# A two-layer trunk on one Trainium2 core: where the values' scale is computed, which queue issues attention's DMAs, and which tile holds a residual

## The chip, the cores and the metric

The kernel runs on one core of a Trainium2 chip. A core has five engines that run their own instruction streams in order and wait for each other by semaphores: TensorE (PE in the profile; PEld is its weight load), VectorE (DVE), ScalarE (ACT), GpSimd (POOL) and SyncE (SP). DMAs are issued by an engine's queue, here SP's or POOL's, and carried out by 16 DMA engines that all queues share. The metric is the device time of one execution in microseconds (us). Matrix products write to PSUM, eight banks, and everything else lies in SBUF or in device memory (DRAM).

## The reference

The function is a trunk of two residual layers over a sequence of 1024 tokens of width 1024, followed by a normalization:

```python
for i in range(DEPTH):                 # DEPTH = 2
    h = rms_norm(x, norm_g[i])
    x = x + (lru_mixer(h, ...) if i == 0 else fox_mixer(h, ...))
return rms_norm(x, final_g)
```

Layer 0 projects `h` to 2 x 1536 columns, runs a causal convolution of four taps, two block-diagonal gates of 12 blocks of 128, and a linear recurrence along the sequence, multiplies by a SiLU gate and projects back. Layer 1 is causal attention with 16 heads of 64 and a forget gate:

```python
u = h @ w_in                           # q, k, v, gate (1024 each), f_logit (16)
cum = cumsum(log_sigmoid(f_logit + b_f))
logits = (q . k) / 8 + cum[query] - cum[key], masked to key <= query
y = softmax(logits) @ v * silu(gate)
x = x + y @ w_out
```

All is float32 in the reference. The kernel keeps close to that by splitting each operand of a product into a high and a low part and adding three products.

## The kernel before, in words

**Tiling and precision.** Activations are held transposed: 128 channels in the partitions, 512 tokens (one half of the sequence) in the free dimension. A weight block is loaded as float32 into a staging tile `wf` (`loaded`, L103: three buffers, and during layer 0 a fourth, `wx`), ScalarE writes its high part `wh` (L88), and GpSimd or VectorE subtracts it to get the low part `wl` (L99); `wh` and `wl` have four buffers each. The staging buffer is free again once the low part is written. `split_weights` (L109) issues these loads on SP's queue (L112), in both layers.

**Layer 0** is a loop of twelve steps (L396 to L440). Step `n` projects one block of 128 recurrence channels, computes the gates of block `n - 1`, the gate branch, the recurrence, and fills in the output projection of earlier pairs of blocks. At its end (L465 to L489) the last pair is projected, the new residual `x1` goes to DRAM (`x1d`), and `rms_row` computes the second norm's row `rs1` and its column form `rms1`, for each half of the sequence.

**Layer 1** starts with the first pair of heads' keys and queries and the first group of values, then loops over 16 heads. A step for head `hd` has two runs: `weigh(hd, 0)` beside `maxima(hd, 1)`, and `weigh(hd, 1)` beside `maxima(hd + 1, 0)`; the second argument is the half of the queries.

- `maxima` (L717) does for each of four blocks of 128 queries: the scores S on TensorE, from a key tile `T[s]` and a query tile `U[s][c]`; mask and maximum on VectorE (L741); the exponential with its sum on ScalarE (L746); the sum divided by a constant on GpSimd (L752) and its reciprocal on VectorE (L753); the weights as two float16 parts `pp`, high on ScalarE (L90) and low on VectorE (L755); and a transposing DMA (L756) of `pp` into `pT[c]`, issued on SP's queue.
- `weigh` (L761) multiplies `pT[c]` by the values into O, once all four transposes have landed. The result is scaled by `tops` (L781 to L783), gated and stored to `y1d`.
- `load` and `load_q` (L624, L636) copy a head's keys and queries, within SBUF, into T and U, and rows of the forget gate from DRAM: four DMAs for T, four for each U, on SP's queue. T and the second U alternate between heads, the first U is shared by all.
- The projections of the next pair (keys, queries, gate) are the `fill` between these steps, six pieces of weights for a pair.
- After every fourth head, `values` (L541) computes the values of the next four heads. They are stored as two float16 parts, so they need a scale that can't overflow. `bound` (L523) finds it: for each of eight weight tiles ScalarE squares the high part times the norm's gain (L528), TensorE sums over partitions with a matrix of ones (`norms`, 128x256 in bfloat16), VectorE takes the maximum over the columns (L531), ScalarE takes a square root (L532), and VectorE derives the inverse, `rv` (L538), and the unit by which O is scaled back. The values' products go on meanwhile, but a finished product can be evicted (L90, L584) only with `rv`.

**The end** starts at head 12. `load_y` (L829) brings back the gated outputs of six pairs, `partial` (L857) multiplies them by the output weights and adds to the residual, which is loaded from `x1d` on SP's queue and stored back to it on GpSimd's (L869). `late` (L952) loads and splits the weights of the last two pairs. `turned` (L889) transposes the residual by TensorE, in quarters of 256 tokens, adds the last two pairs' product in the same PSUM tile, and normalizes. For its first quarter, `residual` (L875) loads into the home of `pT[0]` and the result goes to the home of the key tile `T[0]`.

**Order.** The program is written as generators that are interleaved by hand (`run`, L810, with the strings ORDER and LAST), TensorE's instructions being chained to that order. Within it a planner orders each engine's instructions ahead of time by its own estimate of their durations. On the chip every engine and every queue takes its instructions strictly in that order: an instruction that waits holds up all that is behind it on its engine, a DMA that waits all that is behind it on its queue.

Of the kernel before, what the change touches and what calls it, by code (L numbers as in the profile page):

```python
# [40 lines left out]
def trunk(ctx: ExitStack, tc: tile.TileContext, xt, w0, wg, wo0, pc, gn, gf, w1, wv, wf, bf, wo1, out):  # L41
# [10 lines left out]

    pe = [None]

    def matmul(*args, **kw):
# [15 lines left out]
    nc.vector.memset(tiny, 1e-30)  # L71
    onesb = const.tile([P, P], BF16, name="onesb")
    nc.vector.memset(onesb, 1.0)
    root = const.tile([P, 1], F32, name="root")
# [34 lines left out]
    def split_weights(src, shape, hi_eng, lo_eng, parts=wpool):  # L109
        wt = loaded(shape)  # L110
        for part, sl in src:
            nc.sync.dma_start(wt[:, :, sl], part)  # L112
# [73 lines left out]
    with ExitStack() as l0:  # L186
# [206 lines left out]


        ys, fill, held = [], iter(()), {}
        for n in range(NB):  # L396
            wu = first[0] if n == 0 else list(weights(w0[n]))
            if n == 1:
                ups = both = [ps.tile([P, HALF], F32, tag="g", name="ups") for h in range(2)]
            else:  # L400
                ups = two_banks("ups")
                both = [ups.rearrange("p a b -> p (a b)")]
                ups = [ups[:, h] for h in range(2)]
            product(ups[0], 0, wu)
            if n == 0:
                gps = held[0] = two_banks("gps")
                product(gps[:, 0], 0, first[1])
                for _ in zip(split_x(1), square_x(1)):
                    pass
                done = norm_row(0)  # L410
            else:
                gates(n - 1)
                if n > 1:
                    with tc.issue_after(state[n - 1]["last"].ins):
                        outputs(n - 2)
            product(ups[1], 1, wu)
            if n == 0:
                product(gps[:, 1], 1, first[1])
                norm_row(1)
# [38 lines left out]
        def mm3(o, w, x, start, stop):  # L458
# [3 lines left out]
            matmul(o, wh, xl, start=False, stop=stop)  # L462

        wl = [w for d0 in range(0, KT, 2) for w in out_weights(NB // 2 - 1, d0)]
        for h, cs in enumerate(halves):  # L465
# [4 lines left out]
            for d0 in range(0, KT, 4):  # L470
# [6 lines left out]
                for db, o in enumerate(pts, d0):  # L477
# [10 lines left out]
                    )  # L488
            rms_row(sums, rs1[h], rms1[h])  # L489


# [5 lines left out]
    with ExitStack() as l1:  # L497
# [24 lines left out]

        def bound(g, parts):  # L523

            row = ps.tile([P, HALF], F32, tag="O", name="norms")[:, :256]
            for k in range(KT):
                sq = at.tile([P, 256], BF16, tag="yo", name="sqw", bufs=2)
                nc.scalar.activation(sq, f32(parts[k][0][:, :256]), AF.Square, scale=gnt[:, 1, k : k + 1])  # L528
                matmul(row, onesb, sq, start=k == 0, stop=k == KT - 1)
            most = const.tile([P, 1], F32, name=f"most{g}")  # L530
            nc.vector.tensor_reduce(most, row, mybir.AxisListType.X, ALU.max)  # L531
            nc.scalar.activation(most, most, AF.Sqrt, bias=tiny, scale=SEQ / TOP / TOP)  # L532
            unit_ = tops[g] = const.tile([P, 1], F32, name=f"unit{g}")
            nc.vector.tensor_scalar(unit_, most, 0.5 / TOP, None, ALU.mult)
            nc.vector.reciprocal(most, most)
            rv = const.tile([P, 8], F32, tag="rv", name="rv", bufs=2)
            for h in range(2):
                nc.vector.tensor_scalar(rv[:, 4 * h : 4 * h + 4], rms1[h], most, None, ALU.mult)  # L538
            return rv

        def values(g):  # L541
# [17 lines left out]
            for st, k in todo:  # L559
# [19 lines left out]
                for a in range(2):  # L579
                    v = vpool.tile([P, 4, HD], FP16, tag=f"v{st}", name=f"v{st}", bufs=2)  # L580
                    src = pt[:, a * P : (a + 1) * P].rearrange("p (b d) -> p b d", b=2)
                    rv_ = rv[:, st : st + 1]
                    to_hi(v[:, 0::3], src, nc.scalar, scale=rv_)
                    nc.vector.scalar_tensor_tensor(v[:, 1:3], src, rv_, v[:, 0::3], ALU.mult, ALU.subtract)  # L584
                    Vs[2 * g + a].append(v)
                if ex:
                    nc.vector.tensor_scalar(fz[:, st], pt[:, 256:], r_, None, ALU.mult)

        tops = {}
        kq = {}  # L590
# [7 lines left out]
        def low(pair):  # L598
            return nc.vector if pair else nc.gpsimd

# [23 lines left out]
        def load(hd, cs=slice(0, SEQ), us=(0, 1)):  # L624

            pair, s = hd // 2, hd % 2
            rows = slice(s * HD, (s + 1) * HD)
            hi, lo = (f32(z[rows, cs]) for z in kq[pair, 1])
            nc.sync.dma_start(f32(T[s][:64, 0, cs]), hi)
            nc.sync.dma_start(f32(T[s][:64, 1, cs]), hi)  # L630
            nc.sync.dma_start(f32(T[s][64:, 0, cs]), lo)
            nc.sync.dma_start(f32(T[s][66:68, 1, cs]), cumd[hd, :, cs])
            for c in us:
                load_q(hd, c)

        def load_q(hd, c):  # L636
            s = hd % 2
            u = U[s][c]
            hi, lo = (f32(z[s * HD : (s + 1) * HD, halves[c]]) for z in kq[hd // 2, 0])
            nc.sync.dma_start(f32(u[:64, 0]), hi)  # L640
            nc.sync.dma_start(f32(u[64:, 0]), hi)
            nc.sync.dma_start(f32(u[:64, 1]), lo)
            nc.sync.dma_start(f32(u[64:66, 1]), cumd[hd, :, halves[c]])

# [72 lines left out]
        def maxima(hd, c):  # L717
# [7 lines left out]
            for i in range(4 * c, 4 * c + 4):  # L725
# [25 lines left out]
                r = sums[:, i : i + 1]  # L751
                nc.gpsimd.tensor_scalar(r, r, 1.0 / TOP, None, ALU.mult)  # L752
                nc.vector.reciprocal(r, r)  # L753
# [7 lines left out]
        def weigh(hd, c, sub=slice(0, HALF)):  # L761
# [18 lines left out]
            r0, r1 = s * HD, (1 - s) * HD  # L780
            to, one = yo[r0 : r0 + HD], tops[hd // 4]  # L781
            nc.scalar.activation(to, O[r1 : r1 + HD], AF.Copy, scale=one[r1 : r1 + HD])
# [3 lines left out]
        def gated(hd, c, sub=slice(0, HALF)):  # L786
# [42 lines left out]
        def load_y(c):  # L829
            for pair in range(6):  # L830
                nc.sync.dma_start(f32(pair_of_y(c, pair)[1]), y1d[c, pair])
            yield from ()
# [24 lines left out]
        def partial(todo):  # L857

            for db, c in todo:
# [15 lines left out]
        def residual(c, q):  # L875

            cs = slice(q * 256, (q + 1) * 256)
            if c == q == 0:
                xs = at.tile([P, KT, 256], F32, tag="pT0", name="x1", bufs=1)
                xs = [xs[:, d] for d in range(KT)]  # L880
                for d, x in enumerate(xs):
                    nc.sync.dma_start(x, x1d[c, :, d, cs])
                return xs
            xs = [wpool.tile([P, 2, 256], F32, tag=("wl", "wh")[q], name="x1") for d in range(4)]
            for d, x in enumerate(xs):
                nc.sync.dma_start(x, x1d[c, :, 2 * d : 2 * d + 2, cs])
            return [x[:, i] for x in xs for i in range(2)]

        def turned(c, q):  # L889
# [62 lines left out]
        def late():  # L952

            for half in range(2):
                wh, wl = (kqpool.tile([P, 8, P], F32R, tag=f"qk{p}{half}", name=f"wo{p}") for p in "hl")
                for b in range(2):
                    wt = wpool.tile([P, 4, P], F32, tag="wf", name="wf", bufs=3)
                    for d in range(2):
                        nc.sync.dma_start(wt[:, 2 * d : 2 * d + 2], wo1[half * 4 + b * 2 + d, :, 6:8])
                    sl = slice(4 * b, 4 * b + 4)  # L960
# [150 lines left out]
```

## Time and profile before

| what | time |
| --- | --- |
| median of three runs | 1130.51 us (1129.42 to 1133.2) |
| the profiled execution | 1140.27 us |
| its span, first to last instruction | 1138.5 us |
| mean granted TensorE clock in it | 0.975 |
| busy: TensorE / its weight loads | 1074.5 / 857.5 us |
| busy: VectorE / ScalarE / GpSimd | 761.8 / 624.9 / 151.9 us |
| DMA: 138.86 MB, of it on GpSimd's queue | 4.20 MB |

A page of the profile has the busy time of each engine, the span in 40 slices with a digit each for the busy tenths (and for the granted clock and the DMA engines' busy share), the DMA queues, the chain of work that ended last, and groups of instructions. A group's row reads: line, engine, operation, output<-inputs, shapes, count | busy us, mean ns of one | idle us before it and what ended that. A waits row reads: who waited <- for whom: total us, times, longest. A stretch's row has its bounds and length, then busy us and count for PE, PEld, DVE, ACT and POOL, then the granted clock, the DMA share and GB/s. Durations of matmuls are modelled and overlap, so a chain's spacing, not the mean of a group, tells what one costs. Layer 0 ends near 450 us; the heads run from some 510 to 1095 us.

### The profile page before, as it was taken

How to read it: one execution, taken by the hardware profiler on the slowest of the kernel's cores; microseconds unless marked ns; L12 is line 12 of the kernel's file. 1: busy time of each engine (PE TensorE's matmuls, PEld its weight loads, DVE VectorE, ACT ScalarE, POOL GpSimd, SP SyncE). 2: the span in 40 equal slices, each digit the busy share in tenths (PEclk: the TensorE clock that was granted, in tenths of full speed). 3: DMA queues.
4: the chain of work that ended last, by engine and by line, in shares of the span. 5: the costliest groups of instructions: out<-in, count | busy, mean ns of one | idle time of the engine just before them, and what ended most of it. 6: DMA issues, size and time to landing. Idle time of an engine off the chain costs nothing. (4 is left out here: it accounts for less than half of the span.)

```text
span 1138.5 us, 14931 instructions
## 1 busy us (share of the span) xinstructions
PE 1074.5 (94%) x5130; PEld 857.5 (75%) x5130; DVE 761.8 (67%) x1314; ACT 624.9 (55%) x1053; POOL 151.9 (13%) x215
## 2 busy tenths in 40 slices
PE   9999999999999999899898899988999889999887
PEld 7788888888888887787676776767767678667666
DVE  7888765677567789558767277772776726576445
ACT  8488344445543647367656366553665536554334
POOL 1321212212021102321010000100001000011100
PEclk9999999999999999999999999998999989999899
DMA  6111111111111114338989448893588933899784
GB/s 233 56 47 50 44 52 51 47 51 42 51 52 42 51 52 144 108 95 175 165 178 191 93 114 171 180 191 87 115 177 176 190 87 90 235 210 214 180 206 184
DMA packets 212610, 138.86 MB, mean 122 GB/s; under 512 B 160660, under 2 KB 175508, under 8 KB 212536
## 3 DMA queue, kind: packets, MB, share of 16 engines
q1 hardware_dynamic: 211256, 133.73, 49.8%
q0 software_dynamic: 1280, 4.20, 1.2%
q8 instruction: 40, 0.66, 0.2%
q14 instruction: 34, 0.28, 0.1%
HBM read 59.11 MB, written 15.86 MB: 66 GB/s over the span
## 5 line engine op out<-in xcount | busy, mean ns | idle before, releaser
L56 PE MATMUL gps<-hh,wh 128*128 128x512 f32 x576 | 236.5, 411 | 1.0 <-DVE qkl L620 1.0
L56 PE MATMUL gps<-hl,wh 128*128 128x512 f32 x576 | 229.0, 397 | 0.0
L56 PE MATMUL gps<-hh,wl 128*128 128x512 f32 x576 | 228.7, 397 | 0.0
L88 ACT CAST wh<-wf 128x512 fp32r<-128x512 f32 (+2 forms) x156 | 94.1, 606 | 141.5 <-PE ops L56 53.5
L99 POOL TENSOR_TENSOR wl<-wf,wh 128x512 fp32r<-128x512 f32 (+1 forms) x60 | 99.8, 1670 | 398.5 <-ACT wh L88 367.1
L56 PEld LDWEIGHTS gps<-hl,wh 128*128 128x128 f32 x576 | 109.6, 190 | 25.7 <-issue 0.5
L56 PEld LDWEIGHTS gps<-hh,wh 128*128 128x128 f32 x576 | 110.0, 191 | 25.2 <-DVE qkl L620 1.2
L746 ACT ACTIVATE p<-S,m 128x128 f32<-128x128 f32 (+7 forms) x128 | 94.4, 738 | 59.8 <-DVE sums L753 25.1
L56 PEld LDWEIGHTS gps<-hh,wl 128*128 128x128 f32 x576 | 110.1, 191 | 20.6 <-POOL wl L99 0.3
L755 DVE SCALAR_TENSOR_TENSOR pp<-p,sums,pp 128x128 f16<-128x128 f32 (+7 forms) x128 | 104.1, 814 | 28.1 <-ACT pp L90 27.2
L90 ACT ACTIVATE pp<-p,sums 128x128 f16<-128x128 f32 (+7 forms) x128 | 97.9, 771 | 27.2 <-DVE sums L753 9.1
L741 DVE CUSTOM_DVE_ANT_0 S<-S,mask 128x128 f32<-128x128 f32 (+7 forms) x128 | 97.3, 761 | 22.5 <-PE S L56 21.0
L752 POOL TENSOR_SCALAR sums<-sums 128x1 f32<-128x1 f32 x128 | 37.8, 295 | 497.2 <-ACT p L746 497.1
L56 PE MATMUL O<-pT,v 128*128 128x512 f16 (+3 forms) x396 | 83.2, 340 | 21.5 <-DMA pT<-pp 21.5
L56 PE MATMUL S<-T,U 96*128 96x512 f32 (+7 forms) x384 | 93.7, 353 | 3.7 <-ACT p L746 3.7
L56 PE MATMUL vps<-wh,hh 128*128 128x256 f32 (+1 forms) x256 | 76.9, 301 | 15.3 <-DVE v L584 11.7
L387 DVE TENSOR_TENSOR x<-x,ops 128x512 f32<-128x512 f32 x80 | 54.1, 683 | 48.5 <-PE ops L56 48.5
L56 PEld LDWEIGHTS <-v 128*128 128x128 f16 x396 | 33.2, 102 | 68.9 <-issue 37.4
L56 PEld LDWEIGHTS S<-T,U 128*128 128x128 f32 (+1 forms) x384 | 68.8, 190 | 19.7 <-ACT p L746 6.9
L56 PE MATMUL ups<-hl,wh 128*128 128x512 f32 x192 | 76.9, 401 | 0.1
L56 PE MATMUL ups<-hh,wh 128*128 128x512 f32 x192 | 76.4, 399 | 0.6 <-ACT hh L90 0.6
L56 PE MATMUL ops<-yh,wh 128*128 128x512 f32 x192 | 76.3, 398 | 0.5 <-DVE x L480 0.5
(185 smaller groups left out, 2105.8 us busy)
## 6 DMA issues: line engine op xcount, KB each, us to landing
wf<-in_w SPq DMA_DIRECT2D x100, 256.0 KB
wf<-in_wo SPq DMA_DIRECT2D x64, 128.0 KB
U<-qkh SPq DMA_DIRECT2D x64, 128.0 KB
T<-qkh SPq DMA_DIRECT2D x28, 256.0 KB
x<-in_xt SPq DMA_DIRECT2D x16, 256.0 KB
x1d<-x SPq DMA_DIRECT2D x16, 256.0 KB
wf<-in_wv SPq DMA_DIRECT2D x16, 256.0 KB
U<-qkl SPq DMA_DIRECT2D x32, 128.0 KB
```

Of the source, the lines that this page charges most:

```text
L56: pe[0] = nc.tensor.matmul(*args, **kw)
L88: nc.scalar.copy(hi, src)
L90: nc.scalar.activation(hi, src, AF.Copy, scale=scale)
L99: return eng.tensor_tensor(lo, src, f32(hi), ALU.subtract)
L387: nc.vector.tensor_tensor(x, x, pt, ALU.add)
L741: nc.vector.tensor_tensor_reduce(S[:, :n], S[:, :n], mask[:, SEQ - n :], -1.0, -NEG, ALU.add, ALU.min, accum_out=m)
L746: seen[0] = nc.scalar.activation(p, S[:, :n], AF.Exp, bias=m, scale=-1.0, accum_out=sums[:, i : i + 1])
L752: nc.gpsimd.tensor_scalar(r, r, 1.0 / TOP, None, ALU.mult)
L755: nc.vector.scalar_tensor_tensor(both[:, :, 1], p, r, both[:, :, 0], ALU.mult, ALU.subtract)
```

## The change

It has five parts.

1. The bound on the values leaves attention. In layer 0, steps 1 to 8 each load two pieces of the values' weights (`vsq`, 16 loads of 256 KB in all, on SP's queue, through the weights' staging buffers) and ScalarE squares each and sums it along the row. At the end of layer 0, `value_bounds` multiplies those sums by the larger of two squared gains, adds over partitions with one product of 128x128 by 128x16, takes the square root and derives `unit_v` and `scale_v` for all four groups; `rv` for all is made behind each half's `rms_row`. `bound` and its calls go, and the bfloat16 ones.
2. All loads of attention go through `fetch`. It is SP's queue until the first values and half of the forget gate are done, and GpSimd's from then on: weights, T and U, the stores of gated outputs, and the loads of outputs and residuals. Transposes, the stores of the forget gate's rows and of the result, and the load of the final gain stay on SP's queue.
3. The low parts of the first pair's weights move from GpSimd to VectorE (`low`).
4. The division of the sums in `maxima` moves from GpSimd to VectorE.
5. The first quarter of the residual is loaded into the home of `T[0]`, and its result goes to that of `pT[0]`: the two are exchanged.

```diff
+    loads_by = [nc.sync]
+
+    def fetch(to, src):
+        loads_by[0].dma_start(to, src)
...
         for part, sl in src:
-            nc.sync.dma_start(wt[:, :, sl], part)
+            fetch(wt[:, :, sl], part)
...
+        vsq = const.tile([P, 4, 4], F32, name="vsq")
+
+        def squares_of_values():
+
+            for g, i in itertools.product(range(4), range(4)):
+                wt = loaded((2, 256))
+                nc.sync.dma_start(wt, wv[g, :, 2 * i : 2 * i + 2])
+                flat = wt.rearrange("p a b -> p (a b)")
+                nc.scalar.activation(flat, flat, AF.Square, accum_out=vsq[:, g, i : i + 1])
+                yield
...
             take(fill, 4)
+            if n:
+                take(vsquares, 2)
...
+        def value_bounds():
+
+            g2 = const.tile([P, KT], F32, name="g2")
+            nc.vector.tensor_tensor(g2, gnt[:, 1], gnt[:, 1], ALU.mult)
+            g2 = g2.rearrange("p (k two) -> p k two", two=2)
+            most = const.tile([P, 4], F32, name="most")
+            nc.vector.tensor_tensor(most, g2[:, :, 0], g2[:, :, 1], ALU.max)
+            nc.vector.tensor_tensor(vsq, vsq, most.unsqueeze(1).to_broadcast([P, 4, 4]), ALU.mult)
+            all_ = ps.tile([P, 16], F32, tag="O", name="vnorm")
+            matmul(all_, onesf, vsq.rearrange("p a b -> p (a b)"), start=True, stop=True)
+            nc.vector.tensor_reduce(
+                scale_v, all_.rearrange("p (a b) -> p a b", b=4), mybir.AxisListType.X, ALU.add
+            )
+            nc.scalar.activation(scale_v, scale_v, AF.Sqrt, bias=tiny, scale=SEQ / TOP / TOP)
+            nc.vector.tensor_scalar(unit_v, scale_v, 0.5 / TOP, None, ALU.mult)
+            nc.vector.reciprocal(scale_v, scale_v)
...
             rms_row(sums, rs1[h], rms1[h])
+            if h == 0:
+                value_bounds()
+            nc.vector.tensor_tensor(
+                rv[:, :, 4 * h : 4 * h + 4],
+                rms1[h].unsqueeze(1).to_broadcast([P, 4, 4]),
+                scale_v.unsqueeze(2).to_broadcast([P, 4, 4]),
+                ALU.mult,
+            )
...
-            rv = bound(g, parts)
...
-                    rv_ = rv[:, st : st + 1]
+                    rv_ = rv[:, g, st : st + 1]
...
         def low(pair):
-            return nc.vector if pair else nc.gpsimd
+            return nc.vector
...
-            nc.sync.dma_start(f32(T[s][:64, 0, cs]), hi)
+            fetch(f32(T[s][:64, 0, cs]), hi)
...
-            nc.sync.dma_start(f32(u[:64, 0]), hi)
+            fetch(f32(u[:64, 0]), hi)
...
-                nc.gpsimd.tensor_scalar(r, r, 1.0 / TOP, None, ALU.mult)
+                nc.vector.tensor_scalar(r, r, 1.0 / TOP, None, ALU.mult)
...
-                nc.sync.dma_start(y1d[c, pair], yo)
+                fetch(y1d[c, pair], yo)
...
-                nc.sync.dma_start(x, x1d[c, :, db])
+                fetch(x, x1d[c, :, db])
...
             if c == q == 0:
-                xs = at.tile([P, KT, 256], F32, tag="pT0", name="x1", bufs=1)
+                xs = tu.tile([P, KT, 256], F32, tag="T0", name="x1")
                 xs = [xs[:, d] for d in range(KT)]
                 for d, x in enumerate(xs):
-                    nc.sync.dma_start(x, x1d[c, :, d, cs])
+                    fetch(x, x1d[c, :, d, cs])
...
             if c == 0:
-                res = tu.tile([P, 2, SEQ], F32, tag=f"T{q}", name="res")
+                if q:
+                    res = tu.tile([P, 2, SEQ], F32, tag="T1", name="res")
+                else:
+                    res = at.tile([P, 2, SEQ], F32, tag="pT0", name="res", bufs=1)
...
+        loads_by[0] = nc.gpsimd
         fill = kq_units(0, ((1, (1,)), (0, (1,))))
         gates1 = forget(1)
```

More of the change, by code (lines that the diff above doesn't have):

```diff
@@ L71, in trunk @@
     nc.vector.memset(tiny, 1e-30)
-    onesb = const.tile([P, P], BF16, name="onesb")
-    nc.vector.memset(onesb, 1.0)
     root = const.tile([P, 1], F32, name="root")
@@ L391, in two_banks @@
             return ps.tile([P, 2, HALF], F32, tag="S", name=name)
+        vsq = const.tile([P, 4, 4], F32, name="vsq")
[6 more added lines that the diff above has]
+                yield
+        vsquares = squares_of_values()
         ys, fill, held = [], iter(()), {}
@@ L462, in mm3 @@
             matmul(o, wh, xl, start=False, stop=stop)
+        rv = const.tile([P, 4, 8], F32, name="rv")
+        unit_v = const.tile([P, 4], F32, name="unit_v")
+        scale_v = const.tile([P, 4], F32, name="scale_v")
+        def value_bounds():
[13 more added lines that the diff above has]
+            nc.vector.reciprocal(scale_v, scale_v)
         wl = [w for d0 in range(0, KT, 2) for w in out_weights(NB // 2 - 1, d0)]
@@ L521, in project @@
                 use(h, pt)
[L523 to L539, printed above, removed]
         def values(g):
@@ L587, in values @@
                     nc.vector.tensor_scalar(fz[:, st], pt[:, 256:], r_, None, ALU.mult)
-        tops = {}
         kq = {}
@@ L628, in load @@
             hi, lo = (f32(z[rows, cs]) for z in kq[pair, 1])
[L629 to L632, printed above, removed]
+            fetch(f32(T[s][:64, 0, cs]), hi)
+            fetch(f32(T[s][:64, 1, cs]), hi)
+            fetch(f32(T[s][64:, 0, cs]), lo)
+            fetch(f32(T[s][66:68, 1, cs]), cumd[hd, :, cs])
             for c in us:
@@ L639, in load_q @@
             hi, lo = (f32(z[s * HD : (s + 1) * HD, halves[c]]) for z in kq[hd // 2, 0])
-            nc.sync.dma_start(f32(u[:64, 0]), hi)
-            nc.sync.dma_start(f32(u[64:, 0]), hi)
-            nc.sync.dma_start(f32(u[:64, 1]), lo)
-            nc.sync.dma_start(f32(u[64:66, 1]), cumd[hd, :, halves[c]])
+            fetch(f32(u[:64, 0]), hi)
+            fetch(f32(u[64:, 0]), hi)
+            fetch(f32(u[:64, 1]), lo)
+            fetch(f32(u[64:66, 1]), cumd[hd, :, halves[c]])
         drain(kq_units(0, ((1, (0,)), (0, (0,)))))
@@ L780, in weigh @@
             r0, r1 = s * HD, (1 - s) * HD
-            to, one = yo[r0 : r0 + HD], tops[hd // 4]
+            to, one = yo[r0 : r0 + HD], unit_v[:, hd // 4 : hd // 4 + 1]
             nc.scalar.activation(to, O[r1 : r1 + HD], AF.Copy, scale=one[r1 : r1 + HD])
@@ L830, in load_y @@
             for pair in range(6):
-                nc.sync.dma_start(f32(pair_of_y(c, pair)[1]), y1d[c, pair])
+                fetch(f32(pair_of_y(c, pair)[1]), y1d[c, pair])
             yield from ()
@@ L885, in residual @@
             for d, x in enumerate(xs):
-                nc.sync.dma_start(x, x1d[c, :, 2 * d : 2 * d + 2, cs])
+                fetch(x, x1d[c, :, 2 * d : 2 * d + 2, cs])
             return [x[:, i] for x in xs for i in range(2)]
@@ L958, in late @@
                     for d in range(2):
-                        nc.sync.dma_start(wt[:, 2 * d : 2 * d + 2], wo1[half * 4 + b * 2 + d, :, 6:8])
+                        fetch(wt[:, 2 * d : 2 * d + 2], wo1[half * 4 + b * 2 + d, :, 6:8])
                     sl = slice(4 * b, 4 * b + 4)
```

## The prediction

> **What bounds the kernel now.** I read the page's busy shares and its slices first, then the stretches, then the waits. The page:
>
> ```profile
> span 1138.5 us, 14931 instructions
> PE 1074.5 (94%) x5130; PEld 857.5 (75%) x5130; DVE 761.8 (67%) x1314; ACT 624.9 (55%) x1053; POOL 151.9 (13%) x215
> PEclk9999999999999999999999999998999989999899
> DMA  6111111111111114338989448893588933899784
> ```
>
> TensorE is busy 1074.5 of 1138.5 us, so at most 64 us of idle time can be won, and beside it the time in which the granted clock was below full. The stretches show where both lie (busy time and count for each engine, then clock, DMA share and rate):
>
> ```profile
> 300.00:450.00 150.00, 149.39 (x650) 120.28 (x649) 117.52 (x145) 83.18 (x111) 21.63 (x14) 1.00 0.20 64
> 514.00:990.00 476.00, 440.85 (x2264) 347.38 (x2263) 300.75 (x675) 271.95 (x532) 31.81 (x108) 0.96 0.73 152
> 990.00:1138.50 148.50, 127.21 (x598) 97.38 (x596) 87.76 (x179) 68.89 (x144) 15.38 (x36) 0.95 0.80 204
> ```
>
> The first layer leaves TensorE 0.6 us idle in 150. Attention leaves 35 us in 476 and the end 21 in 148, both at a lower clock. So only what TensorE waits for after 450 us counts, and the waits name it (total, times, longest):
>
> ```profile
> PE O L56 <- DMA pT<-pp: 21.5, 10, 3.6
> PE vps L56 <- DVE v L584: 11.7, 3, 3.9
> PE ops L56 <- ACT wh L88: 5.5, 1, 5.5
> PE turn L56 <- DMA x<-x1d: 4.5, 1, 4.5
> PE vps L56 <- DVE fz L587: 3.6, 1, 3.6
> ```
>
> **The change part by part.** *1. The bound leaves attention.* Each of the four calls to `values` ends its first half like this in the chain that ended last (start, length, what):
>
> ```profile
> 929.34 0.14 PE norms L56
> ...
> 930.03 1.28 ACT L532
> ...
> 932.05 0.24 DVE rv L538
> ...
> 934.24 13.56 PE vps L56 x96
> ```
>
> TensorE stands from 930.3 to 934.2 because the values' PSUM tiles are full and can't be evicted before the factor `rv` exists; 1.28 us of that is the load of the square root's table. Four such stalls are 3.6 + 11.7 = 15.3 us. The 32 `norms` matmuls go as well, at 0.14 us each in the chain: 4.5 us, and with them 1.7 us in which they waited:
>
> ```profile
> L56 PE MATMUL norms<-sqw,onesb 128*128 128x256 bf16 x32 | 8.5, 280 | 1.7 <-ACT sqw L528 1.5
> L90 ACT ACTIVATE v<-vps,rv 128x128 f16<-128x128 f32 x64 | 20.3, 373 | 34.2 <-PE vps L56 24.1 <-DVE v L584 7.4 <-DVE rv L538 2.7
> L584 DVE SCALAR_TENSOR_TENSOR v<-vps,rv,v 128x128 f16<-128x128 f32 x64 | 20.0, 345 | 30.6 <-ACT v L90 30.6
> ```
>
> After each of the four stalls the granted clock is halved for a few us; the first and the last of the four stretches (what is lost is length times 1 - clock):
>
> ```profile
> 480.45:484.60 4.15, 4.15 (x22) 4.02 (x22) 1.05 (x6) 0.10 (x1) 0.00 (x0) 0.59 0.00 0
> ...
> 934.24:938.60 4.36, 4.36 (x20) 4.36 (x21) 0.63 (x3) 0.24 (x1) 0.00 (x0) 0.50 0.01 4
> ```
>
> 1.7 us is lost in the first and 2.2 in the last, 7.0 over the four. Together 15.3 + 4.5 + 1.7 + 7.0 = **28.5 us gained**. What is late next there is the eviction itself: two on ScalarE and two on VectorE for a tile, 2 x 0.373 + 2 x 0.345 = 1.4 us, against 24 matmuls of TensorE, of which 96 take 13.56 us at the partly halved clock (3.4 us for 24; 2.8 without the 2.2 us lost to the clock). It keeps ahead, so no new stall stands there.
>
> *2. The bound enters the first layer.* Sixteen loads of 256 KB, 4.2 MB, go into a stage whose DMA share is 0.20. Sixteen squares of 128x512 with an accumulator on ScalarE are, by the nearest rows, 0.62 us and 0.19 us each:
>
> ```profile
> L169 ACT ACTIVATE sq<-x 128x512 f32<-128x512 f32 x16 | 9.9, 618 | 1.1 <-DVE yl L99 1.1
> L746 ACT ACTIVATION_READ_ACCUMULATOR p<-S,m 128x1 f32 x128 | 24.6, 192 | 0.0
> ```
>
> That is 13 us of ScalarE, which is busy 83 of 150 us there. Each load also passes through one of the weights' staging buffers on SP's queue, ahead of the gates' weights. I take nothing: the split weights have four buffers of each half, so TensorE's next ones lie ready, and its 0.6 us of idle time in 150 says so. The upper end is a loss of 13 us if every square delayed a weight's split; a gain is excluded, since TensorE has no idle time there. The 128x16 product and its six small operations at the layer's end would be 0.9 us at the 0.154 us of a small one (row in part 3) if TensorE stood still for all of them; it has matrix work of the second half, so I take 0.5.
>
> *3. GpSimd's small work goes to VectorE.* The division of the sums was on GpSimd, and VectorE waited for it. One 128x1 operation on VectorE is 0.154 us:
>
> ```profile
> DVE sums L753 <- POOL sums L752: 25.8, 37, 1.8
> L534 DVE TENSOR_SCALAR unit<-most 128x1 f32<-128x1 f32 x4 | 0.6, 154 | 2.9 <-ACT most L532 2.9
> ```
>
> 128 x 0.154 = 19.7 us of work come to VectorE, and 25.8 us of its waiting go: nothing net in attention, where it is busy 301 of 476 us. Near 1000 us, where the loaded outputs are split, it is nearly full; eight such operations cost 1.2 us there. The weights' low halves of the first pair, some ten of 0.66 us, move to VectorE before attention has filled it: nothing.
>
> *4. Loads by GpSimd's queue.* Every load and store of attention but transposes leaves SP: 48 + 16 + 8 weights, 12 of values, 188 of key and query tiles, 60 of outputs and residuals, some 330 by the code's loops. GpSimd shows such issues already (its group, and the landing that the line's own answer gives):
>
> ```profile
> L869 POOL DMA_DIRECT2D x1d<-xp x16 | 9.4, 589 | 46.4 <-DVE xp L868 41.0 <-DVE sums L753 5.4
> ...
> DMA to landing us min/median/max: 2.3/4.1/7.8
> ```
>
> 346 x 0.589 = 204 us of the 624 that are left, a third of the engine. A queue takes one at a time, so a head's 21 loads are 12.4 us if they stand in a row. A key tile's slack (SP's issues, then TensorE's first use):
>
> ```profile
> 538.00 0.65 SPq L629 DMA_DIRECT2D T<-qkh  x1
> ...
> 543.01 1.48 SPq L631 DMA_DIRECT2D T<-qkl  x1
> ...
> 558.37 0.49 PE L56 MATMUL S<-T,U 128*128 128x256 f32 x2
> ```
>
> It is issued by 544.5 and used at 558.4: 13.9 us, some 10 after a landing in 4.1, so a load may come later by that much for nothing. I take 0; the loss has no small upper end (the rivals).
>
> Does SP, with transposes alone, feed TensorE's ten waits for them sooner? Six of the ten, behind odd heads, are long, and the clock is halved after each; the first and the last of the six stretches, and then the 16 us ahead of the first:
>
> ```profile
> 569.03:573.40 4.37, 4.37 (x13) 2.54 (x14) 0.75 (x1) 0.72 (x1) 0.00 (x0) 0.61 0.69 163
> 908.82:914.70 5.88, 5.88 (x14) 3.05 (x15) 0.75 (x1) 1.12 (x2) 0.00 (x0) 0.50 0.64 137
> 553.00:569.00 16.00, 12.48 (x60) 9.46 (x58) 13.77 (x32) 11.32 (x23) 1.50 (x6) 1.00 1.05 175
> ```
>
> The clock's loss over the six is 11 us (1.7 in the first, 2.9 in the last), so up to 21.5 + 11 = 32.5 us lie here. But in the 16 us ahead of the first the DMA engines' share is 1.05: the transposes end late because the engines are full, and the same bytes move after the change. From another queue loads can go between them instead of behind. I take 0, with the ends -32.5 and +18: twelve half-heads, each later by the 1.5 us that two query loads of 128 KB, which stood behind the last transpose, take at the row's 175 GB/s.
>
> *5. Two stalls at the end.* SP's rows around them:
>
> ```profile
> 1043.89 7.93 SPq L756 DMA_TRANSPOSE pT<-pp  x2
> 1051.92 0.52 SPq L112 DMA_DIRECT2D wf<-in_wo  x1
> ...
> 1090.83 4.30 SPq L756 DMA_TRANSPOSE pT<-pp  x1
> 1095.17 3.55 SPq L882 DMA_DIRECT2D x<-x1d  x7
> ```
>
> and the stretches behind the two stalls:
>
> ```profile
> 1056.54:1061.50 4.96, 4.96 (x12) 3.82 (x13) 3.15 (x9) 2.47 (x6) 0.80 (x2) 0.50 0.48 109
> 1098.73:1102.50 3.77, 3.77 (x12) 2.57 (x13) 0.15 (x1) 0.47 (x1) 0.00 (x0) 0.55 0.91 271
> ```
>
> TensorE waits 5.5 us up to 1056.5 for a weight whose load stood behind 7.9 us of transposes, and 4.5 us up to 1098.7 for a residual behind 4.3 us of one. With their clocks they cost 5.5 + 2.5 = 8.0 and 4.5 + 1.7 = 6.2. Both leave that queue; the residual also gets a key tile's home, last read long before by head 14's scores. In return the loads share the engines with the transposes that they overtake. The ends are 0 and 14.2; I take 12, near the upper, since what they waited for was the queue's order.
>
> Sum: 28.5 - 0.5 - 1.2 + 12 = 38.8 us. The profiled execution took 1140.27 us, 9.8 above the median of three runs, 1130.51. 1140.27 - 38.8 is 1101.5; scaled by 1130.51 / 1140.27 it is **1092 us**.
>
> **The rivals.** *B, the transposes come sooner too.* For it: SP's own issue of a transpose took up to 4.3 us beside loads. Against: the share of 1.05. Time: 1092 - 32 = 1060.
>
> *C, the end doesn't improve*, since the transposes' bytes, not the queue's order, delay those loads: 1104.
>
> *D, loads by GpSimd come late, and it is slower.* Stores of the residual wait on that queue for VectorE (41.0 us over the run), and loads for buffers that TensorE frees late; whatever stands behind waits too. A late load costs what the one at 1056.5 cost, 8.0 us with the clock. 38.8 / 8.0 = 4.9, so from five such events on the gain is gone; with eight it is 1156. Against: the 10 us of slack, and a queue a third full.
>
> *E, GpSimd and VectorE hold each other.* The 128 divisions, now on VectorE, may fall into GpSimd's issues of 0.589 us, which fill a third of the time: 128 x 1/3 x half of 0.589 is 12.6 us on the softmax's path: 1104. In the stretch from 990 us, where GpSimd issued 16 stores and VectorE was busy for 88 of 148 us, those issues kept to 0.589. The Trainium skill, "SBUF — State Buffer", section "Who interferes with whom", says that an operation such as `tensor_scalar` in a two-port mode and GpSimd lock each other out of the port pair for whole instructions, which also stops the writing of DMA descriptors; that is what would make E, and no row here shows it.
>
> *F, the bound's stall stays in another form*, the evictions being the limit: only the matmuls, half the stalls and the end are won, some 20 us, 1111.
>
> **How the numbers follow.** A measurement here tells 0.3%, 3.4 us. Forecast 0.52, B 0.15, C 0.08, D 0.16, E 0.06, F 0.03. D gives slower 0.14 and no change 0.02, F 0.01 of no change; faster is 0.83. The forecast's own range is 1080 to 1106 (the end 0 to 14, the first layer to 13). The range that leaves out D's larger part and the last of B is 1062 to 1127.
>
> **What would show it.** Right: no `norms`, no wait of `vps` for `v` or `fz`, no halved clock near the values; TensorE without idle time up to 450 us; waits of `O` for `pT` still near 21 us; the waits of `ops` for `wh` and of `turn` for `x` gone. Wrong: TensorE's `S` or `gps` waiting for DMAs issued by GpSimd (D), gaps before VectorE's 128x1 operations (E), or `O` no longer waiting (B).

## The result, and the profile after

The changed kernel takes 1237.4 us (median of four runs, 1236.65 to 1242.0). The kernel before took 1131.86 us beside it. The ratio is 1.0925, with a 95% interval of 1.086 to 1.0991: the change makes the kernel slower by about 105 us, where 39 us less were forecast.

The page of the kernel after, the lines that answer to those of before:

```profile
span 1235.9 us, 14925 instructions
PE 1069.4 (87%) x5100; PEld 850.6 (69%) x5100; DVE 776.4 (63%) x1439; ACT 613.9 (50%) x1044; POOL 278.3 (23%) x409
...
q0 software_dynamic: 21648, 63.06, 23.5%
```

TensorE's busy time fell by 5.1 us (1074.5 to 1069.4), but its idle time rose from 64.0 to 166.5 us (span less busy). Together that is the difference of the spans, 97.4 us. Of the traffic, 63 MB now runs on GpSimd's queue (q0, "software"), where 4.2 MB did. The stretches of the kernel after (busy time and count of each engine, then clock, DMA share and GB/s):

```profile
300.00:450.00 150.00, 149.39 (x651) 120.80 (x650) 112.92 (x140) 83.75 (x109) 19.82 (x12) 1.00 0.19 62
514.00:990.00 476.00, 353.02 (x1757) 273.64 (x1756) 256.29 (x638) 209.64 (x408) 99.97 (x190) 0.88 0.77 123
...
553.00:569.00 16.00, 12.72 (x61) 9.73 (x59) 12.45 (x33) 9.45 (x18) 7.40 (x14) 1.00 1.03 125
569.00:590.00 21.00, 0.00 (x0) 0.00 (x0) 2.13 (x6) 2.41 (x5) 2.67 (x5) 0.54 1.14 141
591.00:608.00 17.00, 17.00 (x74) 12.57 (x73) 10.15 (x21) 6.54 (x12) 2.12 (x4) 0.90 0.24 57
```

In the 476 us of attention TensorE stands for 123 us, against 35 before. From 569 to 590 us it does nothing at all, while the DMA engines are full. Then it runs on, and they are at 0.24. The 553 to 569 stretch moved 175 GB/s before and moves 125 now, at the same share. What TensorE waits for (total, times, longest), in the kernel after:

```profile
PE O L60 <- issue: 142.9, 14, 24.5
PE ops L60 <- DVE xp L893: 3.0, 1, 3.0
...
PE ops L60 <- DVE sums L777: 1.9, 1, 1.9
PE ops L60 <- ACT wh L90: 1.7, 1, 1.7
PE ups L60 <- ACT wh L90: 1.7, 1, 1.7
```

The waits for values are gone, and so is that of `turn` for its residual. One large one is left, and it has grown sixfold and more: the first product of `O`, 21.5 us before, 142.9 now. "issue" means that the row names no releaser; the answer for the transposes' own line names them for 119.8 of the 142.9 us. That line in the kernel after, over the whole run:

```profile
L781 SPq DMA_TRANSPOSE pT<-pp x128: 1167/1518/14187, 515.5 to 1193.0; - x128
...
  ACT pp L92: 131.2, 30
...
  PE O L60: 119.8, 7
...
DMA to landing us min/median/max: 2.5/5.9/25.1
```

The first row has the shortest, the middle and the longest time that SP needs to issue one (ns). Before, the same row read:

```profile
L756 SPq DMA_TRANSPOSE pT<-pp x128: 1173/1505/4631, 518.1 to 1090.8; - x128
```

The middle is nearly the same; the longest went from 4.6 to 14.2 us. ScalarE waits as well, 131.2 us, for a buffer `pp` that a transpose hasn't read yet. What stands in the way is on GpSimd's queue, here ahead of the stall at 569 to 590 us:

```profile
553.62 0.52 POOL L57 DMA_DIRECT2D T<-qkh  x1 [3.76 <-PE S L60]
...
556.37 0.58 POOL L57 DMA_DIRECT2D wf<-in_w  x1
...
561.48 0.52 POOL L57 DMA_DIRECT2D U<-qkh  x1 [3.48 <-DMA T<-qkh]
...
566.99 0.58 POOL L57 DMA_DIRECT2D y1d<-yo  x1 [0.90 <-DMA wf<-in_w]
```

SP issues the last four transposes of head 1 at 553.3, 556.7, 561.8 and 573.8 us; the last two take 12 us each to issue. The third has landed 25.1 us after its issue began, at 586.9, the fourth at 590.2, and TensorE goes on at 590.3:

```profile
561.82 24.18 SPq L781 DMA_TRANSPOSE pT<-pp  x2
...
590.27 1.87 PE L60 MATMUL O<-pT,v 128*128 128x512 f16 x4 [24.55 <-issue]
```

From 553.6 to 576 us GpSimd issues three key loads, nine query loads, two weights and a store, 2.75 MB by the sizes of the loads (256 KB, 128 KB for queries). These keys are head 3's, and its scores begin only here:

```profile
610.41 0.49 PE L60 MATMUL S<-T,U 128*128 128x256 f32 x2
```

So key loads that are needed more than 50 us later, 25 of them the stall itself, went ahead of transposes that TensorE needed at once, and query loads, weights and the store went with them. The kernel before issues three key loads among these transposes too, on SP's queue at 553.0, 555.4 and 558.7 us, but only one query load with them: 0.92 MB by the time the last transpose is issued, where it is 2.75 MB now. The packets of both queues from 556 to 580 us in the kernel after (packets, MB, share of the 16 engines' time):

```profile
q0 software_dynamic: 834, 2.37, 78.7%
q1 hardware_dynamic: 3035, 0.76, 30.3%
```

and of the 16 us ahead of the same stall in the kernel before:

```profile
q1 hardware_dynamic: 7192, 2.78, 104.1%
```

SP's queue got through 450 packets a microsecond before and 126 after. Nearly all of those before are small: 6863 of the 7192 are under 512 bytes.

### The profile page after: what moved, and what is told of

The parts are those of the page before. It is cut to its first block, busy times and chain, and to the rows that moved or that the text cites. A ratio compares the mean times of both kernels' runs of the same rounds, so it can differ in the third digit from the quotient of the medians.

```text
span 1235.9 us, 14925 instructions
## 1 busy us (share of the span) xinstructions
PE 1069.4 (87%) x5100; PEld 850.6 (69%) x5100; DVE 776.4 (63%) x1439; ACT 613.9 (50%) x1044; POOL 278.3 (23%) x409
## 5 line engine op out<-in xcount | busy, mean ns | idle before, releaser
L60 PE MATMUL O<-pT,v 128*128 128x512 f16 (+3 forms) x396 | 86.7, 350 | 143.9 <-issue 142.9
L92 ACT ACTIVATE pp<-p,sums 128x128 f16<-128x128 f32 (+7 forms) x128 | 97.4, 772 | 150.9 <-DMA pT<-pp 131.2
L101 POOL TENSOR_TENSOR wl<-wf,wh 128x512 fp32r<-128x512 f32 (+1 forms) x50 | 86.4, 1736 | 379.8 <-ACT wh L90 286.0
L101 DVE TENSOR_TENSOR wl<-wf,wh 128x512 fp32r<-128x512 f32 x106 | 70.2, 667 | 13.6 <-ACT wh L90 13.5
L60 PE MATMUL ups<-hh,wl 128*128 128x512 f32 x192 | 76.8, 400 | 0.9 <-POOL wl L101 0.9
```

Source lines behind the costliest of these rows:

```text
L60: pe[0] = nc.tensor.matmul(*args, **kw)
L92: nc.scalar.activation(hi, src, AF.Copy, scale=scale)
L101: return eng.tensor_tensor(lo, src, f32(hi), ALU.subtract)
```

## Experiments

**The theory.** On SP's queue a load stood behind the transposes issued before it. On a queue of its own nothing holds it back, so as soon as its buffer is free it takes the DMA engines from the transposes of the same half-head. **The rivals:** the division on VectorE and GpSimd's issues hold each other up (the prediction's E); loads come late (D); or GpSimd's DMAs slow transposes by their kind, in whatever order they come. All ratios are to the kernel before, with 95% intervals.

**1. Only the queue undone.** All five parts, but `fetch` stays on SP's queue to the end. (The planner then also orders some instructions of the other engines differently, so that this run alone doesn't separate the queue from the order.)

```diff
-        loads_by[0] = nc.gpsimd
```

> The changed kernel with all of attention's loads back on SP's queue (part 2 undone), the other four parts kept. Theory T (loads issued by GpSimd overtake the transposes that TensorE waits for, and the DMA engines serve the two queues by turns, a software packet of 4096 bytes against a transpose's of 256): the six waits of O of 17 to 25 us go back to 2.5 to 3.6, and the time falls to 1095 to 1110 us, below the kernel before. Rival V (VectorE's 128 added small operations, or VectorE and GpSimd locking each other): stays above 1200. Rival L (the loads and squares added to the first layer, or the new home of the residual): stays above 1150.

1108.72 us, ratio 0.9787 (0.9735 to 0.984). TensorE's wait in that run:

```profile
PE O L60 <- DMA pT<-pp: 25.4, 12, 5.1
```

The queue costs 1.0925 - 0.9787 = 0.114 of 1131 us, some 129 us, and the 128 divisions on VectorE, which are still there, cost nothing that can be seen.

**2. The queue without the rest.** The kernel before, with `fetch` on GpSimd's queue and the small work on VectorE; the bound and the residual's home as before.

```diff
+        loads_by[0] = nc.gpsimd
...
-            return nc.vector if pair else nc.gpsimd
+            return nc.vector
...
-                nc.gpsimd.tensor_scalar(r, r, 1.0 / TOP, None, ALU.mult)
+                nc.vector.tensor_scalar(r, r, 1.0 / TOP, None, ALU.mult)
```

> The kernel before with parts 2, 3 and 4 alone: loads by GpSimd's queue, and GpSimd's small work on VectorE; the bound stays in attention, the residual in its old home. T: all of the loss without part 1's gain, 1131 + 105 + 28, so 1245 to 1270 us, with waits of O of 15 us and more behind odd heads. L: about 1131. If the bound's stall gives the transposes time to land, the two losses overlap and it is nearer 1235.

1279.73 us, ratio 1.1318 (1.1245 to 1.1392), 10 us above the range that was expected:

```profile
PE O L60 <- issue: 140.2, 14, 21.8
PE vps L60 <- DVE v L588: 11.7, 3, 3.9
```

The same wait of `O` stands beside the values' stalls of before, so the bound has nothing to do with it.

**3. The bound alone.** The kernel before with the bound in the first layer; nothing else.

```diff
+            if n:
+                take(vsquares, 2)
...
-            rv = bound(g, parts)
```

> Part 1 alone: the bound in the first layer; queues, GpSimd's work and the residual's home as in the kernel before. By the sum on record: 28 us gained, 1100 to 1106 us, no wait of the values' products for v, no idle TensorE in the first layer beyond 1 us. L: slower than before, with gaps of TensorE before 450 us.

1107.15 us, ratio 0.9768 (0.9716 to 0.982): 26 us gained, a time 1 us above the range that was expected, and as much as run 1 within the intervals. The rest of the change, left on SP's queue, is worth nothing.

```profile
PE O L60 <- DMA pT<-pp: 24.6, 12, 3.9
...
PE turn L60 <- DMA x<-x1d: 2.2, 3, 1.7
PE ops L60 <- ACT wh L90: 2.1, 1, 2.1
```

The two stalls at the end are 2.1 and 2.2 us here, 5.5 and 4.5 before, though no queue was changed.

**4. and 5. Which loads.** In run 4 the copies into T and U stay on SP's queue and all other loads go by GpSimd; in run 5 it is the other way round.

```diff
-            fetch(f32(T[s][:64, 0, cs]), hi)
+            nc.sync.dma_start(f32(T[s][:64, 0, cs]), hi)
...
```

> The changed kernel with the key and query tiles' loads (T and U, 188 of 330, some 1.5 MB a head) back on SP's queue behind the transposes, and weights, outputs and residuals (some 0.9 MB a head) on GpSimd's. T: what overtakes is the smaller part, so the long waits of O shrink to 4 to 9 us and the time is 1120 to 1165. If only the loads within SBUF do the harm: 1095 to 1110. V: above 1200.

```diff
-            fetch(f32(T[s][:64, 0, cs]), hi)
+            tu_by[0].dma_start(f32(T[s][:64, 0, cs]), hi)
...
-        loads_by[0] = nc.gpsimd
+        tu_by[0] = nc.gpsimd
```

> The complement of e4: the key and query tiles' loads alone (T and U) on GpSimd's queue, all other loads on SP's behind the transposes. The two halves' losses against e1 (1109 us) should add up to about that of the whole (1237, 128 us): e4 lost 49, so this one loses 70 to 90 and takes 1175 to 1200 us with waits of O of 8 to 14 us behind odd heads, if the loss goes by the bytes that overtake. If it needs both kinds together: 1110 to 1150.

1157.88 us, 1.0243 (1.018 to 1.0305), and 1184.1 us, 1.0435 (1.0371 to 1.0499). Run 4's wait, and run 5's two:

```profile
PE O L60 <- DMA pT<-pp: 60.4, 14, 9.3
```

```profile
PE O L61 <- issue: 47.3, 4, 17.6
PE O L61 <- DMA pT<-pp: 31.5, 9, 14.6
```

Against run 1 they lose 0.046 and 0.065, in sum 0.110, and the whole queue 0.114: both kinds of load do it, and the losses add.

**6. Every load behind the landed transpose.** As the kernel after, but each load by `fetch` up to head 11 waits until GpSimd has read one element of the last transpose issued before it. Same queue, same bytes; only the order is that of one queue again.

```diff
+                if i == 7 and hd < 12:
+                    landed[0] = nc.gpsimd.tensor_scalar(seen_last, f32(turned_[:, 0, 0, 3 * P : 3 * P + 2]), 1.0, None, ALU.mult)
...
+            with tc.issue_after(landed[0].ins):
+                loads_by[0].dma_start(to, src)
```

> The changed kernel, all loads on GpSimd's queue as there, but up to head 11 a one-element operation of GpSimd reads the second half's last transposed block, and the loads that the program gives out behind it stand behind it on that queue: they can't overtake the transposes that TensorE waits for next. Queue, packets and bytes stay. T (overtaking is the cause): waits of O behind odd heads fall from 17 to 25 us to 5 or less, and the time to 1100 to 1150 us; what remains comes from loads that are then late, seen as waits of S or gps. If software-issued DMAs harm by themselves (slower transfers, a busy GpSimd): stays above 1200.

1272.71 us, ratio 1.123 (1.1164 to 1.1297), where 1100 to 1150 us were expected: its time was missed by far. But the waits changed places:

```profile
PE gps L66 <- ACT wh L96: 141.8, 13, 18.8
...
PE O L66 <- issue: 4.4, 2, 2.3
...
ACT wh L96 <- DMA wf<-in_w: 102.6, 24, 13.1
```

`O` waits 4.4 us in place of 142.9. The weights, held back with the rest, are now what comes late, in the way that the prediction's D feared for loads on a queue that waits. Order moves the wait; the number of bytes and the kind of DMA didn't change.

**7. Another engine's queue.** As run 4, but the weights, outputs and residuals go by ScalarE's queue.

```diff
-        loads_by[0] = nc.gpsimd
+        loads_by[0] = nc.scalar
```

> As e4 (T and U on SP's queue), but weights, outputs and residuals go by ScalarE's queue in place of GpSimd's. If any second queue lets loads overtake transposes, waits of O of 5 to 9 us as in e4 stay, 1150 to 1200 us, plus stalls of ScalarE's own work behind loads that wait for their buffers. If the software queue's packets of 4096 bytes are what starves the transposes, the transposes that run beside a load land sooner than in e4, and waits of O are under 4 us, though ScalarE's stalls may cost as much.

1136.91 us, ratio 1.0014 (0.9978 to 1.0051), below the 1150 to 1200 us that were expected, but worse than run 1 by 0.023:

```profile
PE O L60 <- DMA pT<-pp: 50.0, 12, 8.2
```

The wait of `O` is near run 4's 60.4 us. A second queue does it even where it isn't GpSimd's, but GpSimd's costs about twice as much (0.046). The reason isn't shown. One difference stands on the two runs' pages: ScalarE's queue took 22272 packets for 34.6 MB, some 1.6 KB each; in run 4 GpSimd's queue took 12032 packets for 38.8 MB, some 3.2 KB each. Larger packets would take more from the transposes if the engines serve the queues by packets; no run changed the packets alone.

**8. Only the end by GpSimd.** The bound, the exchanged homes, and the loads that the two end stalls waited for (the last weights and the residual) on GpSimd's queue.

```diff
-                    nc.sync.dma_start(x, x1d[c, :, d, cs])
+                    nc.gpsimd.dma_start(x, x1d[c, :, d, cs])
...
-                        nc.sync.dma_start(wt[:, 2 * d : 2 * d + 2], wo1[half * 4 + b * 2 + d, :, 6:8])
+                        nc.gpsimd.dma_start(wt[:, 2 * d : 2 * d + 2], wo1[half * 4 + b * 2 + d, :, 6:8])
```

> Part 1 as in e3, part 5 (the residual's first quarter in the key tile's home), and GpSimd's queue for the residual's and the last two pairs' weights' loads alone, at the very end where few transposes are left. By the prediction's part 5, the waits of ops for a weight and of turn for the residual (2.1 and 1.7 us in e3) go: 1100 to 1105 us, against 1107 of e3. If loads overtake the last heads' transposes: 1107 to 1115.

1110.64 us, ratio 0.9788 (0.9718 to 0.9858): no better than run 3, and not the 1100 to 1105 us that part 5's account gave. The wait of `turn` is gone from its rows, and that of `O` is larger by as much and more:

```profile
PE O L60 <- DMA pT<-pp: 31.0, 15, 3.9
```

**9. The opposite.** If loads that aren't needed yet cost time when they overtake transposes, holding them further back on SP's own queue should gain. The bound alone (run 3), and the copies into T and U are issued on SP's queue only after the last transpose of the second half of the head that was last there.

```diff
+            with tc.issue_after(turned_last[0].ins):
+                nc.sync.dma_start(to, src)
...
-            nc.sync.dma_start(f32(T[s][:64, 0, cs]), hi)
+            behind(f32(T[s][:64, 0, cs]), hi)
...
+                if i == 7:
+                    turned_last[0] = turn_
```

> The bound in the first layer, every load on SyncE's queue, and the next head's key and query loads held in the program's order until after the last transpose of the head before. Theory (loads that are not needed yet overtake the transposes that are, and even on one queue a head's keys stand ahead of some of them): the waits of O for pT behind odd heads, 2.4 to 3.9 us in the run of the bound alone, fall to 1 to 2 us with a part of the halved clock behind them, and the time falls from that run's 1107 us to 1080 to 1100 us, 0.955 to 0.97 of the kernel before. Rival (on one queue the transposes set their own pace and the loads' place doesn't matter): 1100 to 1115 us, ratio 0.97 to 0.985, O's waits as they were. Third: the keys then come late and S waits for them, ratio above 0.985.

1090.7 us (six runs, 1088.58 to 1094.67), ratio 0.9621 (0.9588 to 0.9655): faster than both kernels and than run 3, whose interval begins at 0.9716. SP's queue at the place of the stall, in run 3:

```profile
552.82 1.07 SPq L57 DMA_DIRECT2D T<-qkh  x1
553.98 2.10 SPq L781 DMA_TRANSPOSE pT<-pp  x1
556.13 1.15 SPq L57 DMA_DIRECT2D T<-qkl  x1
...
558.75 5.38 SPq L781 DMA_TRANSPOSE pT<-pp  x2
```

and in run 9:

```profile
553.63 1.56 SPq L789 DMA_TRANSPOSE pT<-pp  x1
...
556.98 4.50 SPq L789 DMA_TRANSPOSE pT<-pp  x2
561.54 1.34 SPq L62 DMA_DIRECT2D U<-qkh  x2
```

The key tiles' loads now come behind, from 570.5 us on, and the wait of 3.6 us here is 0.4. All over the run:

```profile
PE O L68 <- DMA pT<-pp: 7.3, 9, 1.7
```

No row of that run has `S` waiting for a key load, and `O` waits 17 us less than in run 3. So the order on one queue was already worth 17 us (0.9768 - 0.9621 of 1131) in run 3's kernel.

**10. Only T and U held back, on GpSimd's queue.** Run 5, with its copies waiting for the landed transpose as in run 6; the weights stay on SP's queue, so nothing else is held.

```diff
+            with tc.issue_after(landed[0].ins):
+                tu_by[0].dma_start(to, src)
```

> Only the key and query loads by GpSimd, as in the run that gave 1184 us, but each head's loads wait until the last transpose ahead of them has landed (GpSimd reads one element of it); weights, outputs and residuals stay on SyncE's queue. Theory (it is the loads' place ahead of the transposes that costs): the waits of O, 13.2, 14.6 and 17.6 us at most in that run, fall below 4 us up to head 11, and the time falls to 1080 to 1125 us, ratio 0.955 to 0.995. Rival (loads made by GpSimd harm the transposes or VectorE in whatever order): the ratio stays above 1.03. Third: the loads come late in turn, S waits for them by 3 us or more for each of twelve heads, ratio 0.99 to 1.04 with waits of S in place of O's.

1137.66 us (ten runs), ratio 1.002 (0.9988 to 1.0052), against run 5's 1.0435. Its two largest waits:

```profile
PE S L69 <- ACT p L780: 39.9, 15, 3.1
PE O L69 <- DMA pT<-pp: 4.8, 4, 1.6
```

`O` waits 4.8 us in place of 78.8, on the same queue, with the same bytes. For these copies that excludes the rival that GpSimd's DMAs harm transposes in any order. The time expected by the theory (below 1125 us) was missed, because `S` now waits in place of `O`, twelve times by about 3 us. The third expectation forecast such waits and a ratio like this one, but by late loads, and these aren't late loads. The second of the twelve: the first score block of that half-head was ready at 565.1 us, and the matmul of the third waits for ScalarE's exponential of an earlier block.

```profile
570.24 0.29 DVE L775 CUSTOM_DVE_ANT_0 S<-S,mask 128x128 f32<-128x128 f32 x1
...
571.20 0.62 PE L69 MATMUL S<-T,U 128*128 128x384 f32 x2 [3.09 <-ACT p L780]
```

TensorE had computed the first two blocks, at 564.6 and 566.3 us, so the keys were there. VectorE masked the first only at 570.2 us, 5.1 us after it was ready, since outputs, weights and gates stood ahead of it in VectorE's order. In front of all twelve stalls this delay is 5.0 to 5.2 us; in run 5 the same operation starts within 0.8 us at the same twelve places. So the planner's new order of VectorE's work made these waits, and no late load did. Without their 36 us the run would lie near 1100 us, by an estimate from these rows, where the theory had it.

## Why the prediction was wrong, point by point

**The step that failed is part 4's**, "From another queue loads can go between them instead of behind", taken at 0 with the ends -32.5 and +18. The +18 named the direction and missed the size. It let only the two query loads that stood behind the last transpose of a half-head go ahead, 1.5 us. But the queue's order had held back far more. At the stall shown, eight query loads, two weights and the store, 1.84 MB, got ahead of the last transpose that had not in the kernel before. At the profile's 125 to 141 GB/s that is an estimated 13 to 15 us of the 21 by which this stall grew (3.6 to 24.5); the rest wasn't separated. The waits behind the six odd heads are 17 to 25 us. The argument "the same bytes move after the change" was right and beside the point: TensorE waits for the transposes, not for the sum of the bytes. The part's cost measured 129 us (run 1 against the kernel after), where it had been put at nothing.

**Rival D** had the right sign and the wrong subject: it made loads late, and they came too early; transposes came late. Neither `S` nor `gps` waits for a load of GpSimd's in the kernel after. B is refuted (`O` waits longer), and so is F: no row has the values' products waiting. C, an end that doesn't improve by the queue, is part 5's answer below. E is not seen: the division on VectorE takes

```profile
L777 DVE TENSOR_SCALAR sums<-sums x128: 132/151/156, 513.5 to 1188.9; 128x1 f32<-128x1 f32 x128
```

at most 0.156 us beside a GpSimd that issues all through attention. The lock named by the Trainium skill, "SBUF — State Buffer", section "Who interferes with whom", is shown by no row of these runs.

**Part 1**, 28.5 us, holds as far as the runs tell: no `norms`, no wait of `vps` for `v` or `fz`, as said, and run 3 gained 26 us. The first layer's cost and the shorter stalls at the end are in that gain, so the part's own share isn't measured.

**Part 2** took 0.5 us and named 13 as the upper end. It rested on the 0.6 us of idle time from 300 to 450 us. The kernel after has kept these 0.6 us, but the stretch lies behind the added work; the squares end before it:

```profile
L405 ACT ACTIVATE wf<-wf x16: 613/632/635, 25.6 to 246.8; 128x512 f32<-128x512 f32 x16
```

Among them, at 105 us, `ups` waits 1.7 us once for a weight's high part, the kind of delay that the upper end was meant for. With 0.9 and 0.5 us beside it and half of a 3.4 us stretch at the halved clock, it is 4.8 us in the kernel after (granted clock 0.76 from 104 to 111 us). In run 3 the waits are the same and the clock there stays at 1.00, which leaves 3.1.

**Part 3**, nothing net, holds (run 1 against run 3).

**Part 5** took 12 of 14.2 us. Both stalls are less than half as long in run 3 without any change of queue, and run 8, with the queue, is no faster than run 3. In the kernel after, `turn` doesn't wait, but `ops` does three times, 3.0, 1.9 and 1.7 us. So the queue was not what these two stalls hung on alone; they moved with what ran ahead of them, and the 12 us weren't a term of their own.

Without part 4 the sum comes near but for part 5 and the first layer: 38.8 less 12 less 4 is 23, and run 1 gained 24 us (0.0213 of 1131). That is partly luck: in run 1 the waits of `ops` and `turn` are 3.9 and 1.6 us, 5.5 and 4.5 before, so a part of the 12 was won, and `O` waits 25.4 us in place of 21.5.

**The clock.** After the stall at 569 to 590 us it stays halved for about 4 us: the stretch from 591 us shows 0.90, 1.7 us lost in 17, no more than behind the 3.6 us stall before.

## What to carry to other kernels

A queue shared by urgent and early DMAs is also a schedule: moving the early ones to a free queue removes the order that held them back, and they will run as soon as their buffers are free. Before moving loads off a queue, list what the moved ones stood behind, ask when each is needed, and charge all bytes that become issuable early against the urgent transfers, not only the next few. If transposes or other urgent transfers set the pace, try holding the early loads behind them on the same queue (run 9) before giving them another.

## What of the hardware was not expected

**Two queues share the engines very unevenly in bytes.** From 576 to 579 us in the kernel after, with both queues at work:

```profile
q0 software_dynamic: 183, 0.54, 82.8%
q1 hardware_dynamic: 239, 0.06, 16.5%
```

In packets they are near even (1.3 to 1), in bytes 9 to 1, since a transpose's packets are 256 bytes and a load's here some 3 KB on average; elsewhere in the same stall it is up to 6 to 1 in packets (430 against 69 from 573 to 576 us). The Trainium skill, "DMA: Bandwidth & Descriptors", section "Queues, rings and completion order", says that an engine goes round the queues that have work, a packet at a time. The trace agrees in that both queues are served side by side. It doesn't show the turns, nor whether the profile's packets are those that the skill means; a count of 6 to 1 isn't turn and turn about. The Trainium skill, "DMA: Bandwidth & Descriptors", section "Issuing engines are not separate DMA queues" says that starting DMAs from several engines only saves the time of issuing them. The trace agrees that they share the engines, but here it didn't only save: it cost 129 us.

**GpSimd's queue also waits for its own loads.** Its issue at 561.48 us stood 3.48 us until a key load issued 8 us earlier had landed, into another tile. `U` waited 40.7 us for other loads of its own kind over the run:

```profile
POOL U L57 <- DMA U<-qkh: 40.7, 18, 4.6
```

A limit on how many may be in flight would look like this; it wasn't tested.

**An issue isn't short when the engines are full**: SP's issue of a transpose took up to 14.2 us beside GpSimd's loads, 4.6 at most before. Since SP issues in order, all that stands behind it on SP's queue waits too.
